# Low parts of weights used last on every tile, and new durations in the planner of a two-layer decoder trunk

## The chip, the cores and the metric

The kernel runs on one core of one Trainium2 chip, in one launch. The metric is the time of an execution on the device in microseconds (us). Three runs of the kernel before took 1206.88, 1209.07 and 1210.11 us; the median is 1209.07 us. The profile is of one more execution.

## The reference

The reference computes two layers of a decoder trunk on 256 tokens of 1024 features in float32. In short:

```python
for l in range(2):
    ada = silu(c) @ ada_w[l] + ada_b[l]                  # 9 vectors of 1024: shift, scale, gate for three sublayers
    h = rms_norm(x, g[0]) * (1 + scale0) + shift0
    x = x + 0.5 * gate0 * ((silu(h @ Wg) * (h @ Wu)) @ Wo)          # 1024 -> 2 x 2816 -> 1024
    h = rms_norm(x, g[1]) * (1 + scale1) + shift1
    p = h @ mix_w_in[l]                                  # 1024 -> 3360
    y = concat(gated_deltanet(p[...]), native_sparse_attention(p[...]))
    x = x + gate1 * (y @ mix_w_out[l])
    h = rms_norm(x, g[2]) * (1 + scale2) + shift2
    x = x + 0.5 * gate2 * ((silu(h @ Wg2) * (h @ Wu2)) @ Wo2)
return rms_norm(x, final_g)
```

The first sublayer and the third are feed-forward layers, with weights of 1024 x 5632 and 2816 x 1024 each. The mixing in between has four heads of a gated delta rule (a short convolution along the tokens, decays, inverses of unit triangles) and eight heads of attention with three branches (compressed keys, selected blocks, a window). The vectors `ada` that set shift, scale and gate are called the conditioning below; their weights are 1024 x 9216 per layer.

## The kernel before

**Products in two parts.** Activations lie with features on partitions and the 256 tokens along a row. A float32 product is made of three fast ones: weights and activations are each split into a high part, rounded to float32r, and a low part, the rest of the subtraction, and high x high, high x low and low x high are added up in a bank of PSUM. The split of the weights is work at run time. Weights come in tiles of 128 x 1024 floats (512 KB; some are smaller) through ten slots `raw`. For each, `produce()` (its lines follow `def load`) makes the high part `hi` with a copy on ScalarE and the low part `lo` with a subtraction on VectorE. Four slots each are there for `hi` and `lo`, so that at most three tiles are split ahead of the one in use. `take()` hands a pair to the products, and keeps the stream going.

**The order of products within a tile.** `split_mm` (L1018) makes three products for one block of 128 x 128 weights: `wh` with the high activations, `wh` with the low ones, `wl` with the high ones. A tile of weights holds eight blocks (four blocks of rows by two feature blocks of the result; six in one tile of three of the feed-forward's output weights), and the three products of a block follow each other. `early_mm` (L1011), for products that do not wait for the norm, has another order of the same three (`wh`, `wl`, `wh`). `split_mm_nat` (L1211) is for projections with tokens on partitions: there the activations are the stationary operand and a row block of weights, up to 512 columns, is the moving one. Its order is high x `wh`, high x `wl`, low x `wh`. The callers are `first_unit`, `ffn_body` (both halves of a feed-forward layer), `nat`, `proj_t`, `main` (inside `mix_body`) and `mix_out`. Two feature blocks of a result share each weight tile, one after the other.

**After the products.** A pair of feed-forward features goes through `ffn_act` (Silu on ScalarE, a product on VectorE `av`, and a split into `aa` on both). Results of output projections are added to the residual `xT` on VectorE, and `norm_add` takes them into the next norm (squares, a sum `nS` on GpSimd, scaled copies `xh` and `xl`).

**The conditioning.** `ada_piece` works on a piece of 1024 x 512 weights, four loads of 512 KB: some of its eight rows are added up on VectorE (`ada`, multiply-adds of 128 x 512), the others are scaled on ScalarE and added on GpSimd (`adb`). The pieces have fixed places in the stream of weights (`ADA_AT`), between the layers' tiles.

**What sets the order.** The kernel is first recorded, not issued. A planner (class `Program`) gives each instruction an estimated duration (`estimate`, L321), walks forward through the recorded program along these times, and picks for each engine the ready instruction with the longest way to the end; tiles get their slots on the walk. A pass backward sets how late each instruction may start, and eight such passes take turns; the order with the earliest estimated end is issued. So the estimates set the order of all five queues, the loads on SyncE among them, and each queue is then worked off in that order. Products that write one bank keep their recorded order; products of different banks may be mixed by the planner. All instructions are issued at one line, L546, so the profile tells them apart by the names of their tiles.

The functions that the diff touches follow; in many of them it only takes comments away.

Of the kernel before, what the change touches and what calls it, by code (L numbers as in the profile page):

```python
# [17 lines left out]
T = 256  # L18
DEPTH = 2
# [28 lines left out]
def const_arrays():  # L48
    """Masks and index patterns that depend on the shapes alone."""
# [39 lines left out]
DMA_START, DMA_DONE, DMA_BYTES, DMA_RING = 1100, 950, 360.0, 8  # L89
REUSE = {"tensor": 94, "vector": 220, "scalar": 300, "gpsimd": 250, "sync": 0}  # L90
PE_FIX, PE_WINDOW = 2.33, 4096 / 1.2
TABLE_LOAD, TABLE_BIAS = 1280, 5000
PASSES = 8
# [16 lines left out]
class Instr:  # L110
    """A recorded instruction."""
# [20 lines left out]
class LogicalTile:  # L132
    """A tile of the recorded program: one use of one of the slots of its tag."""
# [85 lines left out]
def wait_end(engine, end, other):  # L219
    """When an engine may reuse the place of a tile that another was done with at end."""  # L220
# [5 lines left out]
class Program:  # L226
# [8 lines left out]
    # -- recording --  # L235
# [17 lines left out]
    def region(self, ap):  # L253
        """(tile, first partition, end, bits of the columns)"""
# [21 lines left out]
    def record(self, engine, fn, args, kw):  # L276
# [6 lines left out]
        for w, r in sorted((u for u in uses if u[1]), key=lambda u: u[0]):  # L283
# [21 lines left out]
        if engine == "tensor":  # L305
            # products keep their order within a bank, as one start flag may stand for several of them
# [14 lines left out]
    def estimate(self, x):  # L321
        """Sets the time that the instruction holds its engine, and that of its transfer."""
# [3 lines left out]
        x.table, x.transfer = None, 0  # L326
        if x.fn == "dma_start":
            size = 4 * out.shape[0] * n
            run = min([size] + [4 * a.ap[-1][1] for a in aps])
            x.transfer = size / DMA_BYTES / min(1, run / 512)  # L330
            x.cost = 475
        elif x.engine == "tensor":
# [1629 lines left out]
```

## Time and profile before

| what | value |
|---|---|
| median of three runs | 1209.07 us (1206.88 to 1210.11) |
| span of the profiled execution, first to last instruction | 1203.7 us (its whole time is not listed) |
| tensor engine, products | 1160.3 us busy, 96%, 9450 products |
| tensor engine, weight loads | 1080.6 us, 90% |
| VectorE | 958.1 us, 80% |
| ScalarE | 669.8 us, 56% |
| GpSimd | 219.6 us, 18% |
| DMA | 259.89 MB, mean 216 GB/s |
| mean granted clock of the tensor engine | 0.995 |

Products are pipelined: one of 256 columns is listed with some 283 ns, while the next starts after some 117 ns. So their count in a stretch says more than the busy time. Weight loads run ahead of their products, and a product that has to wait shows first as a weight load that waits. A wait is put down to the operation that ended last before it.

### The profile page before, as it was taken

Reading aid. Unit: us, or ns where it says so; the run is one execution under the profiler, and the core shown is the slowest. Engines: PE = TensorE matmul, PEld = TensorE weight load, DVE = VectorE, ACT = ScalarE, POOL = GpSimd, SP = SyncE. Lnnn points to the kernel's source line nnn. Section 1 sums busy time; section 2 is a strip of 40 time slices with the busy share of each in tenths; the row PEclk is TensorE's granted clock in tenths of the full one; section 3 lists DMA queues with packets and bytes.
Section 4 is the critical chain, followed back from the end, with each engine's and each line's share of the span. In section 5 each row is a group of like instructions: output and inputs, shape, how many; then the busy total and the mean of one; then the engine's idle time right before and its main releaser. Section 6 shows DMA issues by size and latency. Waiting matters only on the chain.

```text
span 1203.7 us, 24132 instructions
## 1 busy us (share of the span) xinstructions
PE 1160.3 (96%) x9450; PEld 1080.6 (90%) x9451; DVE 958.1 (80%) x1716; ACT 669.8 (56%) x1177; POOL 219.6 (18%) x184
## 2 busy tenths in 40 slices
PE   8998989999999999999999999999999999999997
PEld 3698989997988899999999999998797879999997
DVE  3699899898987699988978877999998669855543
ACT  2456446555585556556545454556657556644444
POOL 2033343220001233113221110233100013200001
PEclk9999999999999999999999999999999999999999
DMA  9879999985424378987976887988562235756540
GB/s 333 292 218 313 293 303 308 287 254 171 132 54 123 118 225 294 301 272 227 319 224 187 284 265 221 314 283 283 157 192 55 71 102 181 255 172 193 181 145 36
DMA packets 230758, 259.89 MB, mean 216 GB/s; under 512 B 16130, under 2 KB 190836, under 8 KB 230644
## 3 DMA queue, kind: packets, MB, share of 16 engines
q1 hardware_dynamic: 230644, 258.35, 68.0%
q8 instruction: 74, 1.21, 0.4%
q14 instruction: 40, 0.33, 0.1%
HBM read 256.09 MB, written 2.23 MB: 215 GB/s over the span
## 4 chain that ended last, share of the span: by engine, by line
PE 72%; DVE 16%; DMA 4%; issue 3%; ACT 3%; POOL 1%; DVEq 0%; POOLq 0%; ACTq 0%; SPq 0%
PE bank L546 72%; DVE lo L546 7%; DVE ada L546 2%; ACT hi L546 2%; DMA raw<-in_ffn_w_out_dram 1%; DMA raw<-in_ada_w_dram 1%; DVE qT L546 1%; DVE aa L546 1%; POOL adb L546 1%; DMA raw<-in_ffn_w_in_dram 1%; DMA w<-in_cmp_w_k_dram 1%; DVE av L546 0%; DVE hl L546 0%; DVE KL L546 0%; DVE Pt L546 0%
## 5 line engine op out<-in xcount | busy, mean ns | idle before, releaser
L546 DVE TENSOR_TENSOR lo<-raw,hi 128x1024 fp32r<-128x1024 f32 (+3 forms) x340 | 420.2, 1254 | 119.6 <-ACT hi L546 86.4
L546 ACT ACTIVATE hi<-raw 128x1024 fp32r<-128x1024 f32 (+3 forms) x340 | 344.6, 1028 | 282.1 <-PE bank L546 233.2
L546 PE MATMUL bank<-hh,lo 128*128 128x256 f32 x1440 | 380.2, 285 | 10.4 <-DVE lo L546 10.3
L546 PE MATMUL bank<-hl,hi 128*128 128x256 f32 x1440 | 385.0, 284 | 0.6 <-DVE hl L546 0.6
L546 PE MATMUL bank<-hh,hi 128*128 128x256 f32 x1440 | 384.0, 283 | 1.6 <-ACT hi L546 1.0
L546 PEld LDWEIGHTS bank<-hh,lo 128*128 128x128 f32 x1440 | 260.2, 189 | 14.4 <-DVE lo L546 13.9
L546 PEld LDWEIGHTS bank<-hh,hi 128*128 128x128 f32 x1440 | 264.1, 189 | 4.7 <-issue 1.7
L546 PEld LDWEIGHTS bank<-hl,hi 128*128 128x128 f32 x1440 | 264.2, 189 | 1.2 <-DVE hl L546 0.8
L546 PE MATMUL bank<-aa,hi 128*128 128x256 f32 x1408 | 247.7, 281 | 2.9 <-ACT hi L546 2.5
L546 PEld LDWEIGHTS bank<-aa,hi 128*128 128x128 f32 x1408 | 212.5, 189 | 3.4 <-ACT hi L546 2.7
L546 PE MATMUL bank<-aa,lo 128*128 128x256 f32 x704 | 188.4, 283 | 8.5 <-DVE lo L546 8.5
L546 POOL TENSOR_TENSOR adb<-adb,raw 128x512 f32<-128x512 f32 x65 | 98.4, 1514 | 305.2 <-ACT raw L546 283.9
L546 PEld LDWEIGHTS bank<-aa,lo 128*128 128x128 f32 x704 | 129.5, 189 | 11.2 <-DVE lo L546 11.1
L546 DVE SCALAR_TENSOR_TENSOR ada<-raw,cond,ada 128x512 f32<-128x512 f32 x131 | 111.1, 848 | 4.5 <-DMA raw<-in_ada_w_dram 3.6
L546 POOL TENSOR_TENSOR nS<-nS,nsq 128x256 f32<-128x256 f32 x42 | 42.5, 1013 | 257.8 <-ACT nS L546 184.6
L546 ACT ACTIVATE aa<-av 128x256 fp32r<-128x256 f32 x88 | 36.0, 412 | 60.7 <-DVE av L546 60.5
L546 POOL TENSOR_TENSOR ada<-ada,adb 128x512 f32<-128x512 f32 x28 | 49.7, 1773 | 104.6 <-DVE ada L546 100.6
L546 PE MATMUL bank<-xl,hi 128*128 128x258 f32 (+1 forms) x224 | 62.3, 293 | 1.3 <-DVE xl L546 1.2
L546 PE MATMUL bank<-xh,hi 128*128 128x258 f32 (+1 forms) x224 | 60.5, 289 | 2.1 <-ACT xh L546 2.1
L546 PE MATMUL bank<-xh,lo 128*128 128x258 f32 (+1 forms) x224 | 61.4, 288 | 0.0
L546 DVE TENSOR_TENSOR aa<-av,aa 128x256 fp32r<-128x256 f32 x88 | 48.5, 554 | 10.9 <-ACT aa L546 10.9
L546 PEld LDWEIGHTS bank<-xl,hi 128*128 128x128 f32 x224 | 41.6, 190 | 7.1 <-issue 4.2
(308 smaller groups left out, 1620.9 us busy)
## 6 DMA issues: line engine op xcount, KB each, us to landing
raw<-in_ffn_w_in_dram SPq DMA_DIRECT2D x172, 512.0 KB, 4.8
raw<-in_ada_w_dram SPq DMA_DIRECT2D x144, 512.0 KB, 4.9
raw<-in_ffn_w_out_dram SPq DMA_DIRECT2D x64, 512.0 KB, 4.6
raw<-in_mix_w_in_dram SPq DMA_DIRECT2D x40, 512.0 KB, 5.0
raw<-in_ffn_w_out_dram SPq DMA_DIRECT2D x32, 384.0 KB, 4.3
raw<-in_mix_w_out_dram SPq DMA_DIRECT2D x8, 512.0 KB, 4.2
raw<-in_mix_w_out_dram SPq DMA_DIRECT2D x16, 256.0 KB, 4.5
raw<-in_mix_w_in_dram SPq DMA_DIRECT2D x8, 408.0 KB, 3.8
```

Of the source, the lines that this page charges most:

```text
L546: r = getattr(getattr(self.tc.nc, x.engine), x.fn)(*map(bind, x.args), **{k: bind(a) for k, a in x.kw.items()})
```

## The change

The diff does three things; it also takes the comments and docstrings of the file away.

First, all products of a weight tile with its high part come before all products with its low part. `split_mm`, `early_mm` and `split_mm_nat` go; `split_products` and `early_products` take a list of jobs for a tile.

Second, `estimate` has other figures: of a transfer (a fixed time per packet and a rate, over 16 engines), of a float32r product (2.2 instead of 2.4 columns per ns), of operations on GpSimd.

Third, the walk forward has three new surcharges: up to 500 ns on a vector operation with two inputs of more than 64 elements on chip while GpSimd is busy by the plan; 100 ns on a product after the tensor engine was idle; 95 ns on a product that uses another number of the array's columns than the one before.

```diff
-DMA_START, DMA_DONE, DMA_BYTES, DMA_RING = 1100, 950, 360.0, 8
+DMA_START, DMA_DONE, DMA_RING = 1100, 950, 8
+PACKET, PACKET_BYTES = 8, 23.5
+REFILL, DIVIDE, SHARED = 100, 95, 500
 ...
-        x.table, x.transfer = None, 0
+        x.table, x.transfer, x.cols = None, 0, 128
+        x.port = (x.engine == "vector" and not psum and sum(free_size(a) > 64 for a in aps[1:]) > 1)
 ...
-            x.transfer = size / DMA_BYTES / min(1, run / 512)
+            x.transfer = size / run * (PACKET + run / PACKET_BYTES) / 16
 ...
-                x.cost = PE_FIX + max(m / 1.2, w / 2.4)
+                x.cost = PE_FIX + max(m / 1.2, w / (2.2 if aps[1].dtype == F32R else 2.4))
+            x.cols = out.shape[0] if x.fn != "transpose" else 128
 ...
-            x.cost = 164 * n + 300 if x.kw.get("op") == OP.pow else 2.1 * n + 150
+            x.cost = 230 * n + 250 if x.kw.get("op") == OP.pow else 2.6 * n + 250
 ...
+            if x.port and clock["gpsimd"] > at:
+                cost += min(SHARED, clock["gpsimd"] - at)
             if x.engine == "tensor":
+                cost += (REFILL if at > clock["tensor"] + 20 else 0) + (DIVIDE if x.cols != cols else 0)
+                cols = x.cols
 ...
-    def split_mm(o, wh, wl, xh, xl, first, last):
-        PE.matmul(o, wh, xh, start=first, stop=False, skip_group_check=True)
-        PE.matmul(o, wh, xl, start=False, stop=False, skip_group_check=True)
-        PE.matmul(o, wl, xh, start=False, stop=last, skip_group_check=True)
+    def split_products(jobs):
+        for o, wh, _, xh, xl, first, _ in jobs:
+            PE.matmul(o, wh, xh, start=first, stop=False, skip_group_check=True)
+            PE.matmul(o, wh, xl, start=False, stop=False, skip_group_check=True)
+        for o, _, wl, xh, _, _, last in jobs:
+            PE.matmul(o, wl, xh, start=False, stop=last, skip_group_check=True)
 ...
+    def early_products(jobs, n=T + 2):
+        for o, wh, _, k in jobs:
+            PE.matmul(o[:, 0:n], wh, nst["xh"][:, k, 0:n], start=k == 0, stop=False)
+            PE.matmul(o[:, 0:n], wh, nst["xl"][:, k, 0:n], start=False, stop=False)
+        for o, _, wl, k in jobs:
+            PE.matmul(o[:, 0:n], wl, nst["xh"][:, k, 0:n], start=False, stop=k == KT - 1)
 ...
-                    for j in range(2):
-                        o, cs = qs[j][:, s * 256:(s + 1) * 256], slice(j * 128, (j + 1) * 128)
-                        for k in range(4):
-                            split_mm(o, wh[:, k, cs], wl[:, k, cs], hh[:, 4 * h + k], hl[:, 4 * h + k],
-                                     h == 0 and s == 0 and k == 0, h == 1 and k == 3)
+                    cut = [slice(j * 128, (j + 1) * 128) for j in range(2)]
+                    split_products([(qs[j][:, s * 256:(s + 1) * 256], wh[:, k, cut[j]], wl[:, k, cut[j]], hh[:, 4 * h + k],
+                                     hl[:, 4 * h + k], h == 0 and s == 0 and k == 0, h == 1 and k == 3)
+                                    for j in range(2) for k in range(4)])
```

The other callers change in the same way.

## Rows read from the trace of the kernel before

**Rows 1.** The page: span, tensor engine's busy time, the chain that ended last.
```profile
span 1203.7 us, 24132 instructions
PE 1160.3 (96%) x9450; PEld 1080.6 (90%) x9451; DVE 958.1 (80%) x1716; ACT 669.8 (56%) x1177; POOL 219.6 (18%) x184
...
PE 72%; DVE 16%; DMA 4%; issue 3%; ACT 3%; POOL 1%; DVEq 0%; POOLq 0%; ACTq 0%; SPq 0%
```
**Rows 2.** Stretches: length, busy us (count) per engine, clock, DMA share, GB/s.
```profile
60.00:210.00 150.00, 140.28 (x1158) 137.28 (x1157) 139.24 (x206) 84.43 (x132) 54.27 (x33) 0.98 0.89 287
210.00:420.00 210.00, 203.69 (x1697) 184.38 (x1696) 176.11 (x422) 128.61 (x272) 29.12 (x32) 1.00 0.55 163
420.00:600.00 180.00, 175.92 (x1462) 172.58 (x1461) 162.71 (x230) 103.54 (x160) 43.45 (x31) 1.00 0.84 272
600.00:840.00 240.00, 233.77 (x1946) 229.83 (x1946) 198.19 (x273) 128.90 (x197) 46.42 (x36) 1.00 0.81 257
...
1050.00:1170.00 120.00, 120.00 (x1023) 119.84 (x1022) 64.01 (x83) 56.77 (x81) 0.00 (x0) 1.00 0.57 176
```
**Rows 3.** Waits: us, times, longest; whole span, then 60:210, 210:600, 600:1050.
```profile
PE bank L546 <- DVE lo L546: 19.1, 26, 2.1
PEld bank L546 <- DVE lo L546: 25.7, 32, 2.3
PEld bank L546 <- ACT hi L546: 4.3, 4, 2.7
...
PEld bank L546 <- DVE lo L546: 8.8, 9, 1.8
PEld bank L546 <- DVE lo L546: 7.2, 9, 2.3
PEld bank L546 <- DVE lo L546: 8.6, 13, 1.1
```
**Rows 4.** Groups by shape: count, busy us, mean ns, idle before.
```profile
L546 DVE TENSOR_TENSOR lo<-raw,hi 128x1024 fp32r<-128x1024 f32 x292 | 372.3, 1292 | 100.0 <-ACT hi L546 73.3 <-PE bank L546 16.8 <-ACT aa L546 3.8
```
**Rows 5.** Groups by shape: what follows a finished bank at a layer's end.
```profile
L546 DVE SCALAR_TENSOR_TENSOR xT<-bank,gate,xT 128x256 f32<-128x256 f32 x32 | 15.0, 471 | 11.4 <-PE bank L546 11.2
L546 ACT ACTIVATE xh<-xT,am 128x256 fp32r<-128x256 f32 x48 | 22.3, 497 | 7.9 <-DVE xT L546 7.1 <-DVE am L546 0.8
```
**Rows 6.** Groups by shape: GpSimd's additions of the conditioning.
```profile
L546 POOL TENSOR_TENSOR adb<-adb,raw 128x512 f32<-128x512 f32 x65 | 98.4, 1514 | 305.2 <-ACT raw L546 283.9 <-DMA raw<-in_ffn_w_in_dram 15.4 <-issue 3.0
```
**Rows 7.** Timeline of VectorE from 168 us: start, duration.
```profile
168.17 1.52 DVE L546 TENSOR_SCALAR ada<-raw,cond 128x512 f32<-128x512 f32 x1
...
171.05 1.77 DVE L546 SCALAR_TENSOR_TENSOR ada<-raw,cond,ada 128x512 f32<-128x512 f32 x1
172.75 0.41 DVE L546 TENSOR_TENSOR av<-sg,bank 128x256 f32<-128x256 f32 x1
173.08 0.74 DVE L546 SCALAR_TENSOR_TENSOR ada<-raw,cond,ada 128x512 f32<-128x512 f32 x1
173.74 0.47 DVE L546 TENSOR_SCALAR ada<-raw,cond 128x512 f32<-128x512 f32 x1
```
**Rows 8.** Timeline of ScalarE from 173 us; in brackets the idle time before.
```profile
173.19 0.42 ACT L546 ACTIVATE aa<-av 128x256 fp32r<-128x256 f32 x1 [3.16 <-DVE av L546]
...
173.78 1.05 ACT L546 ACTIVATE hi<-raw 128x1024 fp32r<-128x1024 f32 x1
```
**Rows 9.** Timeline of the tensor engine from 174 us.
```profile
174.88 0.50 PE L546 MATMUL bank<-aa,hi 128*128 128x256 f32 x2 [2.48 <-ACT hi L546]
...
177.09 0.58 PE L546 MATMUL bank<-hh,lo 128*128 128x256 f32 x1 [1.59 <-DVE lo L546]
```
**Rows 10.** Slices of 5 us from 170 us, columns as in rows 2.
```profile
170.00:175.00 5.00, 2.52 (x22) 2.31 (x21) 5.00 (x7) 1.66 (x4) 3.23 (x3) 1.00 0.51 135
175.00:180.00 5.00, 3.41 (x16) 3.21 (x17) 5.00 (x8) 0.00 (x0) 0.34 (x1) 0.54 1.05 343
180.00:185.00 5.00, 5.00 (x42) 4.85 (x40) 3.48 (x5) 3.88 (x7) 0.95 (x1) 0.78 1.08 359
```

More of the change, by code (lines that the diff above doesn't have):

```diff
@@ L451, in forward @@
         window, cold, busy = 0, True, {}
+        cols = 128
         while len(order) < len(self.instrs):
@@ L1009, in norm_modulate @@
         return hh, hl
-    def early_mm(o, wh, wl, k, n=T + 2):
-        xh, xl = nst["xh"][:, k, 0:n], nst["xl"][:, k, 0:n]
-        PE.matmul(o[:, 0:n], wh, xh, start=k == 0, stop=False)
-        PE.matmul(o[:, 0:n], wl, xh, start=False, stop=False)
-        PE.matmul(o[:, 0:n], wh, xl, start=False, stop=k == KT - 1)
-    def split_mm(o, wh, wl, xh, xl, first, last):
-        PE.matmul(o, wh, xh, start=first, stop=False, skip_group_check=True)
-        PE.matmul(o, wh, xl, start=False, stop=False, skip_group_check=True)
-        PE.matmul(o, wl, xh, start=False, stop=last, skip_group_check=True)
+    def early_products(jobs, n=T + 2):
[10 more added lines that the diff above has]
+            PE.matmul(o, wl, xh, start=False, stop=last, skip_group_check=True)
     def ffn_act(f, g, bias, up, ah, al):
@@ L1046, in first_unit @@
                 wh, wl = take(("fi", l, i, u), 2 * h + s)
-                for k in range(4):
-                    for j in range(2):
-                        cs = slice(j * 128, (j + 1) * 128)
-                        early_mm(qs[j][s], wh[:, k, cs], wl[:, k, cs], 4 * h + k, T if startup else T + 2)
+                cut = [slice(j * 128, (j + 1) * 128) for j in range(2)]
+                early_products([(qs[j][s], wh[:, k, cut[j]], wl[:, k, cut[j]], 4 * h + k) for k in range(4) for j in range(2)],
+                               T if startup else T + 2)
         gu = tmp([128, 2, 2, T], F32, "gu")
@@ L1092, in ffn_body @@
                     wh, wl = take(("fi", l, i, u), 2 * h + s)
-                    for j in range(2):
-                        o, cs = qs[j][:, s * 256:(s + 1) * 256], slice(j * 128, (j + 1) * 128)
-                        for k in range(4):
-                            split_mm(o, wh[:, k, cs], wl[:, k, cs], hh[:, 4 * h + k], hl[:, 4 * h + k],
-                                     h == 0 and s == 0 and k == 0, h == 1 and k == 3)
+                    cut = [slice(j * 128, (j + 1) * 128) for j in range(2)]
+                    split_products([(qs[j][:, s * 256:(s + 1) * 256], wh[:, k, cut[j]], wl[:, k, cut[j]], hh[:, 4 * h + k],
+                                     hl[:, 4 * h + k], h == 0 and s == 0 and k == 0, h == 1 and k == 3)
+                                    for j in range(2) for k in range(4)])
             for j in range(2):
@@ L1107, in ffn_body @@
                     wh, wl = take(("fo", l, i, u, kh), c)
-                    for j in range(2):
-                        cs = slice(j * 128, (j + 1) * 128)
-                        for k in range(a, b):
-                            f = kh * 11 + k
-                            split_mm(qs[j][:, 0:256], wh[:, k - a, cs], wl[:, k - a, cs], ah[f], al[f], f == 0, f == NF - 1)
+                    cut = [slice(j * 128, (j + 1) * 128) for j in range(2)]
+                    split_products([(qs[j][:, 0:256], wh[:, f - kh * 11 - a, cut[j]], wl[:, f - kh * 11 - a, cut[j]], ah[f], al[f],
+                                     f == 0, f == NF - 1) for j in range(2) for f in range(kh * 11 + a, kh * 11 + b)])
             for j in range(2):
@@ L1203, in nat @@
                 wh, wl = take((tag, l), j)
+                tok = [slice(b * 128, (b + 1) * 128) for b in range(2)]
                 for k in range(2):
                     for b in range(2):
-                        t = slice(b * 128, (b + 1) * 128)
                         kk = 2 * j + k
-                        split_mm_nat(qs[b][:, :n], hh[:, kk, t], hl[:, kk, t], wh[:, k], wl[:, k], kk == 0, kk == KT - 1)
-            return qs
-        def split_mm_nat(o, xh, xl, wh, wl, first, last):
-            PE.matmul(o, xh, wh, start=first, stop=False)
-            PE.matmul(o, xh, wl, start=False, stop=False)
-            PE.matmul(o, xl, wh, start=False, stop=last)
+                        PE.matmul(qs[b][:, :n], hh[:, kk, tok[b]], wh[:, k], start=kk == 0, stop=False)
+                        PE.matmul(qs[b][:, :n], hl[:, kk, tok[b]], wh[:, k], start=False, stop=False)
+                for k in range(2):
+                    for b in range(2):
+                        kk = 2 * j + k
+                        PE.matmul(qs[b][:, :n], hh[:, kk, tok[b]], wl[:, k], start=False, stop=kk == KT - 1)
+            return qs
         def proj_t(tag, j):
@@ L1219, in proj_t @@
                 wh, wl = take((tag, l), 2 * j + h)
-                for c in range(2):
-                    o = q[:, c * 256:(c + 1) * 256]
-                    for k in range(4):
-                        cs = slice(c * 128, (c + 1) * 128)
-                        split_mm(o, wh[:, k, cs], wl[:, k, cs], hh[:, 4 * h + k], hl[:, 4 * h + k],
-                                 h == 0 and c == 0 and k == 0, h == 1 and k == 3)
+                cut = [slice(c * 128, (c + 1) * 128) for c in range(2)]
+                split_products([(q[:, c * 256:(c + 1) * 256], wh[:, k, cut[c]], wl[:, k, cut[c]], hh[:, 4 * h + k], hl[:, 4 * h + k],
+                                 h == 0 and c == 0 and k == 0, h == 1 and k == 3) for c in range(2) for k in range(4)])
             return q
@@ L1258, in main @@
                     wh, wl = take(("k", l), 2 * h + j)
-                    for k in range(4):
-                        for c in range(2):
-                            early_mm(qs[2 * j + c], wh[:, k, c * 128:(c + 1) * 128], wl[:, k, c * 128:(c + 1) * 128], 4 * h + k)
+                    cut = [slice(c * 128, (c + 1) * 128) for c in range(2)]
+                    early_products([(qs[2 * j + c], wh[:, k, cut[c]], wl[:, k, cut[c]], 4 * h + k) for k in range(4) for c in range(2)])
             rb = nst.pop("rbs")
@@ L1860, in mix_out @@
                 wh, wl = take(("mo", l, u), j)
-                for c in range(2):
-                    cs = slice(c * 128, (c + 1) * 128)
-                    for k in range(4):
-                        split_mm(qs[j][:, c * 256:(c + 1) * 256], wh[:, k, cs], wl[:, k, cs], yh[:, 4 * u + k], yl[:, 4 * u + k],
-                                 u == 0 and c == 0 and k == 0, u == 1 and k == 3)
+                cut = [slice(c * 128, (c + 1) * 128) for c in range(2)]
+                split_products([(qs[j][:, c * 256:(c + 1) * 256], wh[:, k, cut[c]], wl[:, k, cut[c]], yh[:, 4 * u + k], yl[:, 4 * u + k],
+                                 u == 0 and c == 0 and k == 0, u == 1 and k == 3) for c in range(2) for k in range(4)])
                 if u == 0:
```

## The prediction

> **What bounds the kernel now.** I read the page first. The tensor engine is busy 1160.3 of 1203.7 us, so 43.4 us is all the time in which it shows nothing to do; the chain that ended last is 72% tensor engine and 16% vector engine [rows 1]. The reader should see that two engines share the bound: a gain can come from the 43.4 us, and only where the vector engine is not the limit itself.
>
> Then the stages. From 1050 to 1170 us, with no conditioning work left, the tensor engine runs 1023 products in 120.00 us, without a gap: 117 ns a product [rows 2]. That is its pace when everything arrives. From 60 to 210 us it makes 1158 products where 150/0.117 = 1282 would fit; there the vector engine is busy 139.24 of 150 us and the DMA engines 0.89 of the time at 287 GB/s. From 420 to 600 us it makes 1462 of 1538, with the vector engine at 162.71 of 180. From 600 to 840 us, 1946 of 2051, the vector engine at 198.19 of 240. The mixing stage (210 to 420 us) has other shapes, so its count says nothing, but its idle time, 6.3 us, is small.
>
> Then the waits. The weight loads, which go ahead of each product, waited 25.7 us for the low parts of weights, 32 times, the longest 2.3 us, and only 4.3 us for the high parts; the products' own share of the wait for low parts is 19.1 us [rows 3]. By stretch the low parts cost 8.8 us (60 to 210), 7.2 us (210 to 600) and 8.6 us (600 to 1050); 1.1 us lies outside these.
>
> **The change: high parts first.** The same products run on the same tiles. No instruction and no byte is added or removed. Of a weight tile's 24 products the first that needs the low part was the third; it becomes the seventeenth. At 117 ns that is 14 x 0.117 = 1.64 us of extra cover for the subtraction that makes the low part, whose mean is 1292 ns [rows 4]. The output projection's tiles of three row blocks have 18 products, and gain 10 x 0.117 = 1.17 us; the token-major projections of the mixing have 12 longer ones, where the first low product moves from second to ninth. The mean wait is 25.7/32 = 0.80 us, so nearly every wait is shorter than the cover; of the longest, 2.3 us, about 0.7 us would stay. If each wait were an accident by itself, some 24 us would go: one end of the term. The other end is nothing: where the vector engine is full, the cover is used up once, the backlog grows on, and the next tile waits instead.
>
> I choose by stretch. From 60 to 210 us the vector engine has 7% to spare and the DMA 11%, so I credit 2 of 8.8 us. In the other two stretches and the remainder (7.2 + 8.6 + 1.1 = 16.9 us) the vector engine has 10 to 17% free, and the waits come singly, so I credit two thirds, 11 us. Term A: -13 us, between -24 and 0. What is late next is the high part: ScalarE's copies and the loads behind them. The high tile comes free after 16 products instead of 24, which helps that copy a little; the low tile and the raw tile come free no earlier.
>
> **What it moves to the end of a unit.** Two feature blocks share each weight tile. Before, the first block's bank was complete 12 products ahead of the second (9 in a tile of three row blocks); now it is 4 ahead (3). Its eviction starts 8 x 0.117 = 0.94 us (0.70 us) later, nearer to the second one's. Within a stage the next unit's products cover that. At the four ends of a feed-forward layer and the two of the output projection of the mixing the next norm waits for both blocks: the addition to the residual (471 ns) and the scaled copy (497 ns) of each now queue behind the other's [rows 5]. At most 4 x 0.70 + 2 x 0.94 = 4.7 us, at least nothing, as the first units of the next layer are started early. Term B: +2 us.
>
> **The estimates.** They cost no time on the chip by themselves; they change the planner's order on all queues, the loads on SyncE among them. The old figures are optimistic on each resource alike: a product 109 ns against 117 measured, now 118.7; a GpSimd addition of 512 columns 1225 ns against 1514 measured [rows 6], now 1581; a load of 512 KB in rows of 1 KB 1456 ns, now 512 x (8 + 1024/23.5)/16 = 1650 ns. Since the products and the loads all slow down by some 10%, most rankings should stay. What is new is the 500 ns that a vector operation with two large inputs on chip pays while GpSimd works.
>
> One place shows what that may be worth. At 171.05 us a multiply-add of the conditioning took 1.77 us, where the same one at 173.08 us took 0.74 [rows 7]; between them sat the product of a feed-forward feature, for which ScalarE waited 3.16 us in its own queue [rows 8], with the next high part behind it. The tensor engine then stood 2.48 us for that high part and 1.59 us for the next low part [rows 9]. After that idling the granted clock was 0.54 for a slice of 5 us, near the lower of its two levels (1.2 of 2.4 GHz), and 0.78 in the next; from 170 to 185 us there are 22 + 16 + 42 = 80 products where 15/0.117 = 128 would fit, 48 x 0.117 = 5.6 us lost [rows 10]. Of that 1.59 us is in term A. A planner that knows the price of the overlap would put the feature's product first. I credit half of the 4 us left, and nothing for all other reorderings, whose worth the trace of one order cannot show; the tensor engine's idle time that is not for low parts (43.4 - 19.1 = 24.3 us [rows 1, 3]) bounds their gain, and two more bursts of 5.6 us are the bound that I take for a loss. Term C: -2 us, between -24.3 and +11.2.
>
> A rule of the Trainium skill bears on this. The row at 168.17 us is a multiplication with one large input, and it took 1.52 us against 0.47 us for the same at 173.74 us [rows 7]; the planner's new surcharge goes to operations with two large inputs alone. The skill's page "SBUF — State Buffer", section "Who interferes with whom", says why both kinds can stretch: GpSimd shares a pair of ports with VectorE, a two-input operation and a one-input multiplication in a two-port mode both want it, and whoever starts first holds it for its whole instruction, so GpSimd is blocked as well. The trace agrees for VectorE, with 1.52 and 1.77 us. By that rule the new estimates still miss a part of the contention, and term C would be 0 instead of -2.
>
> **Sum.** -13 + 2 - 2 = -13 us on the profiled span of 1203.7 us, so a span of about 1190.7 us. The median of the runs, 1209.07, lies 5.4 us over that span (the page gives no other time of that execution); with the same 5.4 us on top, **1196 us**. With A between -18 and -6, B between 0 and +4 and C between -4 and +2, its own range is 1188 to 1204.
>
> **Rivals.**
> *The vector engine is the bound* (15%). The waits for low parts only move to later tiles. For it: 93% busy from 60 to 210 us [rows 2], and its 16% of the chain [rows 1]. Against it: from 600 to 840 us it has 17% free and the waits are as dear, 8.6 us from 600 to 1050. It would give about 3 us net: 1206, no change.
>
> *Slower: conditioning loads ahead of weights* (14%). The planner now thinks that a load of weights takes 13% longer, and reorders the loads. A piece of the conditioning is 4 loads of 512 KB, 2.1 MB; at 350 GB/s (343 and 359 in the fullest slices [rows 10]) it holds the weights behind it up by 6 us. It decides where the ten raw tiles on chip, 5.2 MB or 15 us of transfers, are full of such pieces when a feed-forward layer needs weights. For it: the DMA engines are 0.89 busy from 60 to 210 us, and 0.84 from 420 to 600 [rows 2]. Against it: weights that the tensor engine needs have the longer way to the end, and only 4.3 us are lost on high parts now [rows 3]. Three such pieces, 18 us, against the 13 gained: 1209 + 5 = 1214.
>
> *The order gets better everywhere* (13%). With right durations the in-order queues stop waiting behind operations that are late. For it: the burst at 170 us. It would take A at its end, -24, and C at -4, without B: 1181.
>
> **Numbers.** The forecast has 58%. The measurement can tell about 0.3%, 3.6 us: faster means under 1205.4, slower over 1212.7. Faster 0.58 + 0.13 = 0.71, the same 0.15, slower 0.14. The range leaves out the farther half of the third rival and most of the second: 1182 to 1211.
>
> **What would show it.** The weight loads' wait for low parts should fall from 25.7 us to under 13, most of the rest before 210 us; the waits for high parts should stay under 8 us; between 60 and 210 us the product count should rise from 1158 by no more than 50, between 600 and 840 us by about 50; no slice near 175 us should show a clock of 0.54. Waits of the weight loads for the scaled copies at the ends of layers should grow, by some 2 us. I am wrong if the low parts' wait falls and other waits of the same size replace it, or if the clock falls in more places.

## The result and the profile after

The changed kernel takes 1219.44 us (median of four runs, 1215.77 to 1220.31) against 1207.97 us for the kernel before in the same session: a ratio of 1.0092, 95% interval 1.0071 to 1.0112. It is slower by about 11 us. The forecast was 1196 us, and 1182 to 1211 with rivals, so it was wrong in sign and in range. The profiles below are of single executions: the changed kernel's took 1219.31 us, 1.8 us more than its span. If the same holds before, 3.6 of the 5.4 us that the forecast put on top of its span were a difference between executions.

The page of the changed kernel, with the lines that answer to [rows 1]:

```profile
span 1217.5 us, 24148 instructions
...
PE 1177.2 (97%) x9450; PEld 1088.9 (89%) x9451; DVE 955.5 (78%) x1716; ACT 672.7 (55%) x1177; POOL 219.7 (18%) x184
...
PE 75%; DVE 13%; DMA 6%; issue 2%; ACT 2%; POOL 1%; SPq 0%; DVEq 0%; POOLq 0%; ACTq 0%
```

The span is 13.8 us longer, and the tensor engine idles less, 40.3 instead of 43.4 us. It is listed as busy 16.9 us longer for the same 9450 products. So the loss does not show as idle time of the engine, which is where all the mechanisms that I had forecast would show it. By the listed lengths (some 283 ns for a product of 256 columns, 117 ns to the next) a wait under some 166 ns is counted as busy.

The stretches of [rows 2], with the same columns:

```profile
60.00:210.00 150.00, 142.99 (x1186) 140.03 (x1185) 143.20 (x209) 86.28 (x134) 56.19 (x34) 0.99 0.89 292
210.00:420.00 210.00, 204.36 (x1631) 179.02 (x1631) 171.62 (x415) 128.25 (x271) 27.88 (x33) 1.00 0.52 156
420.00:600.00 180.00, 177.10 (x1472) 173.53 (x1472) 157.42 (x228) 101.03 (x155) 37.66 (x28) 1.00 0.83 271
600.00:840.00 240.00, 233.89 (x1930) 229.35 (x1930) 192.38 (x266) 128.08 (x193) 49.91 (x36) 0.99 0.79 255
...
1050.00:1170.00 120.00, 120.00 (x1014) 119.84 (x1014) 69.36 (x94) 56.98 (x83) 1.29 (x1) 1.00 0.62 196
```

From 60 to 210 us there are 28 products more than before, and from 1050 to 1170 us the pace is nearly the same, 120/1014 = 118 ns a product. From 210 to 420 us there are 66 fewer. From 600 to 840 us, where I had expected about 50 more, there are 16 fewer.

The waits of the weight loads, as in [rows 3]:

```profile
PEld bank L558 <- issue: 35.3, 120, 0.8
PEld bank L558 <- DVE lo L558: 13.8, 26, 1.2
...
PEld bank L558 <- ACT hi L558: 5.7, 8, 1.2
PEld bank L558 <- POOL nS L558: 5.0, 4, 2.2
```

The low parts cost 13.8 us instead of 25.7. "Issue", where nothing that the profile shows was awaited, is the largest row. It was so before, with a line that [rows 3] leaves out:

```profile
PEld bank L546 <- issue: 28.1, 86, 1.7
```

It grew by 7.2 us, all in the two mixing stages (17.8 us before, 25.2 after), and `nS` grew by 4.7 us from 0.3. Together that is as much as the low parts' wait fell.

I then cut both traces at places that mean the same in each: the start of the last output product of a layer's first feed-forward part (tiles `aa`), and the start of the last product of the mixing's output projection (tiles `yh`, `yl`). The two mixing stages of the kernel before:

```profile
250.11:424.15 174.04, 170.20 (x1416) 151.28 (x1415) 144.59 (x388) 112.34 (x252) 17.18 (x24) 1.00 0.46 134
821.80:1002.44 180.64, 176.22 (x1414) 152.21 (x1413) 148.29 (x384) 115.55 (x256) 23.53 (x22) 1.00 0.47 138
```

and of the changed one:

```profile
240.61:424.44 183.83, 178.22 (x1416) 152.93 (x1415) 148.31 (x394) 114.60 (x255) 18.90 (x26) 1.00 0.44 132
820.62:1015.45 194.83, 187.04 (x1415) 157.88 (x1413) 154.05 (x393) 117.04 (x258) 25.36 (x24) 0.97 0.43 130
```

The mixing went from 174.0 + 180.6 = 354.7 us to 183.8 + 194.8 = 378.7 us, 24.0 us more. All the rest went from 849.0 to 838.9 us, 10.1 us less, 9.5 of these in the first feed-forward layer. The number of products in the two stages is the same (2830 and 2831); the tensor engine's listed busy time in them rose by 18.8 us and its idle time by 5.1 us.

The granted clock is 0.97 in the second of these stages, 1.00 before. It stood at 0.50, the lower of its two levels (1.2 of 2.4 GHz), from 824.6, 851.9 and 903.1 us for 3.4 us each; in the 4 us ahead of each the engine was busy 2.3 to 2.7 us. At half speed 10.2 us cost at most 5.1 us, an estimate.

A part of the longer busy time can be seen in one group, the products of the attention's probabilities with the values. They use 64 of the array's 128 columns. Before:

```profile
L546 PE MATMUL bank<-pt,vp 128*64 128x128 f32 x192 | 20.7, 287 | 2.1 <-ACT pt L546 2.1
```

After:

```profile
L558 PE MATMUL bank<-pt,vp 128*64 128x128 f32 x192 | 28.8, 293 | 0.0
```

192 products of 64 columns occupy 8.1 us more. The timeline of the tensor engine in the first mixing stage shows what stands between them. Before:

```profile
359.88 0.65 PE L546 MATMUL bank<-pt,vp 128*64 128x128 f32 x6
360.46 0.70 PE L546 MATMUL bank<-qT,kT 128*128 128x256 f32 x2
361.09 0.43 PE L546 MATMUL bank<-pt,vp 128*64 128x128 f32 x2
361.45 0.49 PE L546 MATMUL bank<-qT,kT 128*128 128x128 f32 x2
361.87 0.66 PE L546 MATMUL bank<-pt,vp 128*64 128x128 f32 x8
362.46 0.81 PE L546 MATMUL bank<-qT,kT 128*128 128x256 f32 x3
```

After:

```profile
354.34 0.38 PE L558 MATMUL bank<-hl,hi 128*128 128x256 f32 x1
354.66 0.43 PE L558 MATMUL bank<-pt,vp 128*64 128x128 f32 x2
355.02 0.39 PE L558 MATMUL bank<-hh,hi 128*128 128x256 f32 x1
355.24 0.39 PE L558 MATMUL bank<-qT,kT 128*128 128x128 f32 x2
355.56 0.43 PE L558 MATMUL bank<-pt,vp 128*64 128x128 f32 x2
355.92 0.33 PE L558 MATMUL bank<-CC,vT 128*128 128x128 f32 x1
356.01 0.37 PE L558 MATMUL bank<-hl,hi 128*128 128x256 f32 x1
356.21 0.27 PE L558 MATMUL bank<-CC,vT 128*128 128x128 f32 x1
356.41 0.43 PE L558 MATMUL bank<-pt,vp 128*64 128x128 f32 x2
356.78 0.33 PE L558 MATMUL bank<-CC,vT 128*128 128x128 f32 x1
```

Before, value products come in runs of six, two and eight: the eight from 361.87 us hand over after 0.59 us. After, pairs stand between single products of 128 columns: the pair at 354.66 us takes 0.36 us until the next product starts, and the one product ahead of it 0.32 us instead of 0.12. Counted along the two mixing stages, two neighbouring products use a different number of columns 175 times before and 217 times after. From start to start these pairs sum to 40.6 us before and 50.8 us after. That is 10.2 of the 24.0 us; the other 13.8 us are in pairs with the same number of columns.

### The profile page after: what moved, and what is told of

The parts are those of the page before. It is cut to its first block, busy times and chain, and to the rows that moved or that the text cites. A ratio compares the mean times of both kernels' runs of the same rounds, so it can differ in the third digit from the quotient of the medians.

```text
span 1217.5 us, 24148 instructions
## 1 busy us (share of the span) xinstructions
PE 1177.2 (97%) x9450; PEld 1088.9 (89%) x9451; DVE 955.5 (78%) x1716; ACT 672.7 (55%) x1177; POOL 219.7 (18%) x184
## 4 chain that ended last, share of the span: by engine, by line
PE 75%; DVE 13%; DMA 6%; issue 2%; ACT 2%; POOL 1%; SPq 0%; DVEq 0%; POOLq 0%; ACTq 0%
PE bank L558 75%; DVE lo L558 6%; DMA raw<-in_ada_w_dram 4%; DVE ada L558 1%; DVE Pt L558 1%; DMA Pt<-nd 1%; ACT hi L558 1%; POOL nS L558 1%; DVE aa L558 1%; DMA raw<-in_ffn_w_in_dram 0%; DMA raw<-in_ffn_w_out_dram 0%; DVE QS L558 0%; DVE qT L558 0%; SPq L558 0%; DVE av L558 0%
## 5 line engine op out<-in xcount | busy, mean ns | idle before, releaser
L558 PE MATMUL bank<-hh,hi 128*128 128x256 f32 x1440 | 354.2, 286 | 5.3 <-ACT hi L558 2.8
L558 PE MATMUL bank<-hl,hi 128*128 128x256 f32 x1440 | 351.0, 285 | 1.2 <-DVE hl L558 1.2
L558 PE MATMUL bank<-hh,lo 128*128 128x256 f32 x1440 | 254.3, 285 | 5.2 <-DVE lo L558 4.9
L558 PEld LDWEIGHTS bank<-hh,lo 128*128 128x128 f32 x1440 | 208.6, 189 | 9.7 <-DVE lo L558 8.1
L558 PE MATMUL bank<-aa,hi 128*128 128x256 f32 x1408 | 210.8, 282 | 1.9 <-ACT aa L558 0.8
L558 PEld LDWEIGHTS bank<-aa,hi 128*128 128x128 f32 x1408 | 188.5, 189 | 3.0 <-ACT aa L558 1.2
L558 PE MATMUL bank<-aa,lo 128*128 128x256 f32 x704 | 129.3, 284 | 2.7 <-DVE lo L558 2.6
L558 DVE SCALAR_TENSOR_TENSOR ada<-raw,cond,ada 128x512 f32<-128x512 f32 x131 | 111.3, 851 | 11.7 <-DMA raw<-in_ada_w_dram 11.0
L558 PEld LDWEIGHTS bank<-aa,lo 128*128 128x128 f32 x704 | 104.2, 188 | 5.2 <-DVE lo L558 4.6
L558 DVE TENSOR_TENSOR aa<-av,aa 128x256 fp32r<-128x256 f32 x88 | 45.9, 525 | 10.7 <-ACT aa L558 10.5
L558 ACT ACTIVATE raw<-raw,cond 128x512 f32<-128x512 f32 x65 | 44.4, 711 | 7.4 <-DMA raw<-in_ada_w_dram 7.2
L558 PE MATMUL bank<-xh,lo 128*128 128x258 f32 (+1 forms) x224 | 46.0, 290 | 0.0
```

Of the source, the lines that this page charges most:

```text
L558: r = getattr(getattr(self.tc.nc, x.engine), x.fn)(*map(bind, x.args), **{k: bind(a) for k, a in x.kw.items()})
```

## The experiments

Three theories. **A**: the order of products (low parts last) hurts the mixing. **B**: the new durations reorder it. **C**: the order of before was a lucky one, and any other order from the planner is slower. All times are medians; ratios are to the kernel before in the same session, with 95% intervals where there were three rounds. "Mixing" is the sum of the two stages cut as above.

**Parts alone.** The old durations with the new order of products:

```diff
-DMA_START, DMA_DONE, DMA_RING = 1100, 950, 8
+DMA_START, DMA_DONE, DMA_BYTES, DMA_RING = 1100, 950, 360.0, 8
 ...
-REFILL, DIVIDE, SHARED = 100, 95, 500
+REFILL, DIVIDE, SHARED = 0, 0, 0
 ...   # and the old formulas of transfer, float32r product and GpSimd
```

> High parts first everywhere, with the planner's estimates of before. The two mixing stages took 174 and 181 us before and 184 and 195 us after the change; the feed-forward layers got 11 us shorter in sum. Theory A (the order of products is what hurts the mixing: with low parts last the tensor engine's queue there gets worse, whatever the durations): the time stays at 1213 to 1221 us, the mixing at 182 or more and 190 or more. Theory B (the new durations reorder the mixing): the mixing goes back to about 174 and 181 us, the feed-forward gain stays, 1193 to 1201 us.

Measured: 1218.56 us, ratio 1.0092 (1.0077 to 1.0107), mixing 367.1. The time is as theory A had it; of the mixing's stages only the first is, with 186.1 us, and the second is as before, with 181.0. The gain outside of the mixing is gone as well (849.5 us against 849.0). One more thing was not expected: the low parts are still waited for.

```profile
PEld bank L558 <- DVE lo L558: 22.8, 29, 1.9
```

The new durations with the products in turn:

```diff
+    def split_in_turn(jobs):
+        for o, wh, wl, xh, xl, first, last in jobs:
+            PE.matmul(o, wh, xh, start=first, stop=False, skip_group_check=True)
+            PE.matmul(o, wh, xl, start=False, stop=False, skip_group_check=True)
+            PE.matmul(o, wl, xh, start=False, stop=last, skip_group_check=True)
 ...   # early_in_turn and nat likewise; all callers use these
```

> The new estimates and surcharges, with the three products of each block in turn as before. Theory A: mixing near 174 and 181 us, no gain in the feed-forward layers, 1204 to 1211 us. Theory B: mixing near 184 and 195 us and no gain in the feed-forward layers, 1218 to 1232 us. The waits of the weight loads for low parts should be near 25 us by both.

Measured: 1212.75 us, ratio 1.0050 (1.0031 to 1.0069), mixing 366.3. Between the two theories' ranges; slower without any new order of products, so B holds in part. The profiled execution, with 1216.54 us, is the slowest of the four, and its clock stood at the lower level for 13.6 us of the mixing, worth at most 6.8 us (estimate, half of the time).

```profile
PEld bank L558 <- DVE lo L558: 25.3, 37, 2.0
```

Then the order of products changed in the feed-forward layers alone. With the new durations (only the mixing's callers use the products in turn):

> As the changed kernel, but in the mixing (its three kinds of projections and its output projection) the three products of a block stay in turn. Theory A: mixing near 174 and 181 us with the feed-forward gain kept, 1193 to 1201 us. Theory B: mixing near 184 and 195 us, 1215 to 1222 us.

Measured: 1203.64 us, 0.9972 (0.9957 to 0.9987), mixing 360.2. A little faster than before, nearer to A than to B. With the old durations:

> High parts first in the feed-forward layers alone, with the old estimates. Both theories: mixing near 174 and 181 us. If the feed-forward gain of 11 us comes from the order, 1195 to 1200 us; if it comes from the estimates, 1206 to 1210 us.

Measured: 1221.14 us, 1.0105 (1.0088 to 1.0122), mixing 366.4, the rest 858.2. Neither case. Here not a line of the mixing or of the durations differs from before, and yet the mixing takes 11.7 us longer. This profile, too, is of the slowest of four executions (1226.47 us): its mixing stages have a clock of 0.96 and 0.98, 20.4 us at the lower level, worth at most 10.2 us by the same estimate. The 14 us by which the median is over before's are not explained by that alone, as the other three executions have a clock of 0.988 to 0.992 against 0.991 to 0.997 before. One order per kernel is not enough to compare kernels that a planner arranges; that led to the next group.

**Other orders of the same kernel.** A fixed number between 0 and 20 ns per instruction is added to the planner's rank:

```diff
-        x.boost = self.boost
+        x.boost = self.boost + (len(self.instrs) * 2654435761 + 1 * 40503) % 65536 / 65536 * 20
```

Of the kernel before, three such orders (1, 2 and 3 in the place of the first 1 behind the sum):

> The kernel before, unchanged but for a number between 0 and 20 ns, fixed per instruction, that is added to the planner's rank, which reaches to a million ns; it breaks near-ties another way. Theory C (the order of before was a lucky or tuned draw, and any other order from the same planner is slower): 1213 to 1225 us, the two mixing stages together 362 us or more instead of 354.6. Theories A and B (the changed parts themselves make the mixing slower): 1204 to 1211 us, mixing 350 to 359 us.

> The same with other numbers of that size. Theory C: 1213 to 1225 us, mixing 362 us or more. Theories A and B: 1204 to 1211 us, mixing 350 to 359 us.

> The same with other numbers of that size. Theory C: 1213 to 1225 us, mixing 362 us or more. Theories A and B: 1204 to 1211 us, mixing 350 to 359 us.

Measured: 1206.63, 1200.43 and 1194.56 us, mixing 357.9, 349.1 and 352.6. Theory C falls: the order of before is rather one of the slower ones. Of the changed kernel:

> The changed kernel with 0 to 20 ns per instruction added to the planner's rank, as in the first of the kernels of before with such numbers. Orders of the kernel before drawn in this way took 1207, 1200 and 1195 us beside its own 1207. If the change itself makes orders slower: 1210 us or more for all three of these, mean near 1216, mixing together 368 us or more. If the change only drew an unlucky order: 1195 to 1216 us with a mean near 1203, mixing 348 to 372 us.

> The same with the second set of numbers. The change is slower by itself: 1210 us or more. An unlucky order: anywhere from 1195 to 1216 us.

> The same with the third set of numbers. The change is slower by itself: 1210 us or more. An unlucky order: anywhere from 1195 to 1216 us.

Measured: 1223.01, 1219.50 and 1218.87 us, mixing 375.4, 374.2 and 376.8. With the first order of each, the kernel before has a mean of 1202.4 us over four orders and the changed one 1220.2; the mixing has 353.6 and 376.3, and no order of one comes near those of the other. The rest of the program is 844.6 and 842.5 us. So the loss is the change's own, about 18 us over orders (17 by the ratios to the kernel before in each session), and lies in the mixing. The lower clock does not make it: with half of the time at the lower level taken off each mixing, the means are 351.9 and 373.3 us, and the orders with number 2, with a clock of 1.00 in all four stages, have 349.1 and 374.2. The gain of 10.1 us outside of it was mostly the luck of one order: over four it is 2 us. Nor is the share of the column changes one of a single order: the pairs across a change sum to 38.3 us before and 51.9 after (means of four), 13.6 of the 22.7 us; the value products take 19.4 to 20.7 us in all four orders before and 28.6 to 28.8 in all four after.

A second order for each part alone:

> High parts first everywhere with the old estimates, in a second order (0 to 20 ns added to the planner's rank). If the order of products is a cause, mixing 363 us or more together and 1210 us or more, as in the first order (367 us, 1218.6). If that was one bad draw, 358 us or less and 1195 to 1208 us.

Measured: 1221.51 us, mixing 370.0.

> The new estimates with the products in turn, in a second order. If the estimates are a cause, mixing 363 us or more and 1208 us or more, as in the first order (366 us, 1212.8). If that was one bad draw, 358 us or less and 1195 to 1207 us.

Measured: 1211.46 us, mixing 359.9: the time as a cause had it, the mixing between the two cases. Over two orders each, the order of products alone costs 17.6 us against the mean of before, the durations alone 9.7 us. The order of products is a cause by these times. For the durations 9.7 us is less than the 13 us by which orders of one kernel differ, so two orders make it likely and no more. Neither part alone does what both do to the columns: there are 192 and 180 changes of column count with the order of products, 174 and 169 with the durations, 147 to 175 before and 217 to 232 with both.

**The changes of column count.** The planner's rank of a product loses 2000 ns where its column count differs from that of the product before:

```diff
-                            key=lambda c: c[1].way + c[1].boost - TABLE_BIAS * switch(c[1]) - IDLE * (c[0] - at))
+                            key=lambda c: c[1].way + c[1].boost - TABLE_BIAS * switch(c[1]) - IDLE * (c[0] - at)
+                            - 2000 * (c[1].engine == "tensor" and c[1].cols != cols))
```

In the changed kernel:

> The changed kernel, where the planner's rank of a product loses 2000 ns if it uses another number of the array's columns than the product before it on the tensor engine. In the mixing stages the changed kernel changes that number 217 times against 175 before, and spends 8.2 us more on such pairs. If these changes of columns are a cause of the loss, they fall to under 150, and the mixing goes from 183.8 and 194.8 us to about 177 and 187: 1202 to 1208 us. If the loss is only waits for other engines in an unlucky order, the count falls and the time stays at 1213 to 1225 us.

Measured: 1197.10 us, 0.9909 (0.9883 to 0.9934), 102 changes in the mixing instead of 217, mixing 355.9. More than was expected. In the kernel before (which gets `cols` as well, and no surcharge):

> The kernel before, where the planner's rank of a product loses 2000 ns if it uses another number of the array's columns than the one before it; durations and products as before. It has 175 such pairs in the mixing. If these pairs cost by themselves, wherever they come from, they fall to under 120 and the mixing from 354.6 to about 348 us: 1197 to 1203 us. If only the changed kernel suffers from them: 1204 to 1210 us.

Measured: 1186.64 us, 0.9818 (0.9799 to 0.9836), 99 changes instead of 175, mixing 340.8. It is faster than both kernels by far, and by more than was expected. Its mixing stages:

```profile
248.90:419.70 170.80, 167.46 (x1414) 151.06 (x1413) 145.46 (x389) 112.00 (x253) 16.22 (x25) 0.99 0.48 137
813.80:983.80 170.00, 165.19 (x1414) 149.76 (x1413) 147.05 (x384) 114.17 (x256) 23.70 (x22) 0.99 0.49 145
```

and those of the changed kernel with the same rank:

```profile
241.64:413.76 172.12, 166.50 (x1414) 150.72 (x1413) 148.17 (x390) 114.06 (x253) 18.49 (x25) 0.99 0.48 140
814.07:997.86 183.79, 174.28 (x1415) 154.43 (x1413) 151.66 (x394) 115.72 (x259) 24.90 (x24) 0.96 0.47 138
```

The value products of this kernel:

```profile
L550 PE MATMUL bank<-pt,vp 128*64 128x128 f32 x192 | 13.6, 280 | 1.4 <-ACT pt L550 1.4
```

and of the changed kernel with the same rank:

```profile
L559 PE MATMUL bank<-pt,vp 128*64 128x128 f32 x192 | 14.7, 282 | 1.7 <-ACT pt L559 1.7
```

From 20.7 and 28.8 us both are now near 14. The reader should see that the tensor engine was "busy" all along in time that could be saved. In both kernels what is saved in the mixing stands in the pairs across a change: they sum to 22.6 us (40.6 without the rank) and 23.7 us (50.8), while all other pairs take some 4 us more in each. The waits "issue" of the weight loads fall with them, from 28.1 and 35.3 to 18.0 and 18.9 us. The two other corners of the square, each part alone with this rank:

> High parts first with the old estimates, the planner keeping to a column count. The corners of the square known so far: neither part 1186.6 us, both parts 1197.1. If the order of products costs beside the column changes: 1194 us or more, mixing 350 us or more (340.8 with neither part). If the estimates make the rest: 1184 to 1189 us.

Measured: 1200.96 us, 0.9940 (0.9924 to 0.9957), mixing 348.1.

> The new estimates with the products in turn, the planner keeping to a column count. If the estimates cost beside the column changes: 1194 us or more, mixing 350 us or more. If the order of products makes the rest: 1184 to 1189 us.

Measured: 1195.80 us, 0.9906 (0.9885 to 0.9928), mixing 347.3. So with most of the column changes out of the way 10.5 us of loss remain (1197.10 against 1186.64), nearly all of the 11.5 us between the two kernels as they were, and either part alone makes about as much or more: 14.3 and 9.2 us. In the mixing the loss falls from 24.0 to 15.1 us, and of these only 1.1 us are left in pairs across a change; the other 14 us are in pairs of one column count, as 13.8 us were without the rank, and have not gone. The parts alone make 7.3 and 6.5 us there, just under what was expected of a cause. All four kernels became faster by 17 to 22 us with this rank, more than the 13 us by which orders of one kernel differ. The differences among the four, from single orders each, are hardly so.

**Who spends the cover.** The plan of the kernel before is kept for all queues; afterwards the places that one weight tile's products hold on the tensor engine are refilled with the high parts first, where no eviction stands in between (186 of 292 tiles):

```diff
-        self.issue(self.schedule())
+        self.issue(self.low_last(self.schedule()))
 ...
+            new = sorted(mine, key=lambda x: (weight(x) is lo, at[x]))
+            spots = [at[x] for x in mine]
 ...   # a tile is left as it is where an operand would not be ready or a place would be reused
+            for x, n in zip(new, spots):
+                order[n], at[x] = x, n
```

> The kernel before, planned as it was; afterwards, for 186 of 292 weight tiles (where no eviction stands in between), the places of the tile's products are refilled, high parts first. Every other queue keeps its order. If the cover is worth something and the planner spends it: the waits of the weight loads for low parts fall from 25.7 to 12 us or less, mixing stays near 354.6, 1194 to 1202 us. If the cover is worth nothing: 1204 to 1211 us, with other waits in the place of those for low parts.

Measured: 1200.47 us, 0.9935 (0.9913 to 0.9956), mixing 357.9, the rest 843.4 instead of 849.0.

```profile
PEld bank L546 <- DVE lo L546: 12.8, 14, 2.0
...
PEld bank L546 <- ACT hi L546: 4.4, 7, 1.4
...
PEld bank L546 <- DVE av L546: 3.4, 2, 1.7
```

The waits for low parts are halved, from 25.7 us in 32 waits to 12.8 in 14, a little short of the 12 us expected, and the kernel is 6.5 us faster than before in its session (1206.93 us). Here the cover, on top of a plan made without it, is worth half of the waits that it takes away. The same on the kernel that keeps to a column count:

> The same refilling, of 183 of 292 tiles, on the kernel before whose planner keeps to a column count (1186.6 us). If the cover is worth something: waits for low parts from 28.3 to 14 us or less and 1174 to 1181 us. If not: 1184 to 1189 us.

Measured: 1185.81 us, 0.9810 (0.9787 to 0.9833). The waits fell as expected, from 28.3 us:

```profile
PEld bank L550 <- DVE lo L550: 11.2, 13, 1.6
```

But the time did not follow: it cannot be told from 0.9818. The rest fell from 843.9 to 839.3 us and the mixing rose from 340.8 to 344.4. Waits for high parts rose from 2.2 to 7.5 us.

## Why the prediction was wrong

**Term A (-13 us): right in its sign in this run, wrong in its mechanism.** The waits fell to 13.8 us, close to the "under 13" that I had named, and the first feed-forward layer got shorter by 9.5 us. But I took the cover of 1.64 us as a gift that stays, as if all other queues kept their order. It is a planner's input. With the order of products changed and the old durations the waits were 22.8 and 18.8 us, against 22.7 to 26.7 in the four orders of before; with both changes they were 13.8, 14.8, 16.0 and 20.6 us; with the same order of products laid over the old plan they were 12.8. So the planner gave back a part of the cover: over four orders 8.3 us of waits went (24.6 to 16.3), not 13. Nor did they go where I had said: from 60 to 210 us, where VectorE is fullest and I credited 2 us, 8.8 us became 3.3, and from 600 to 1050 us 8.6 became only 6.5. I also priced a microsecond of wait as a microsecond of time. Outside of the mixing the four orders gained 2 us, and in the two refilled kernels 12.9 and 17.1 us of waits gave 6.5 us and nothing clear of noise. Taking the k-th high part and the k-th low part of the trace, the low part was ready 2581 ns (mean) after the high one in the kernel before, 2865 ns in the refilled one, 3445 ns in the one planned with low parts last and old durations, and 3430 ns in the changed one. The row that answers to [rows 4] shows the same shift. After:

```profile
L558 DVE TENSOR_TENSOR lo<-raw,hi 128x1024 fp32r<-128x1024 f32 x292 | 372.8, 1288 | 102.1 <-PE bank L558 66.0 <-ACT hi L558 26.5 <-issue 4.4
```

Before, VectorE's idle time ahead of a subtraction ended mostly with its high part (73.3 of 100.0 us): it waited for it. Now it ends mostly with a product (66.0 of 102.1 us). A subtraction reads the raw and the high tile, so a product that it waits for is one that sets a low tile free. A low tile comes free at the end of its products, as before; the high one now comes free earlier, and the wait moved from one to the other. In the refilled kernel:

```profile
L546 DVE TENSOR_TENSOR lo<-raw,hi 128x1024 fp32r<-128x1024 f32 x292 | 371.9, 1291 | 90.1 <-ACT hi L546 46.5 <-PE bank L546 29.0 <-issue 5.8
```

it is in between. That the high tile comes free earlier I had named, but I put no price on it. What else the planner did with the cover is not shown.

**Term B (+2 us): not tested by itself, and its sign did not show.** The waits of the weight loads for the scaled copies `xh`, which I had expected to grow by some 2 us, fell from 3.9 to 0.8 us; those for the sum of squares `nS` at the ends of layers grew from 0.3 to 5.0 us. The refilled kernels leave tiles as they were where an eviction stands in between, so they do not test it.

**Term C (-2 us, between -24.3 and +11.2): the step that failed.** I wrote that the product durations and the loads all slow by some 10% so that most rankings should stay, and that the mixing's "other shapes" say nothing while "its idle time, 6.3 us, is small". I gave "nothing for all other reorderings", and no term at all to what the new order of products does to the plan. The mixing is where the new order decides. Its loss of 24.0 us in this run (22.7 over orders) is beyond my bound for a loss, 11.2 us, which I had set at two more bursts like the one at 175 us. Idle time was the wrong measure there: only 5.1 us of the 24.0 are listed as idle time.

About half of the loss is known: the new plan mixed products of 64 and 32 columns with those of 128. In pairs of neighbours with different column counts the time from start to start summed to 40.6 us before (175 pairs) and to 50.8 us after (217), 10.2 us more and not the 8.2 us that I name in an expectation above; over four orders it is 13.6 of 22.7 us. Keeping to a column count takes that part away, 24.0 us become 15.1. The rest stays, and its cause is open. The changed kernel's surcharge DIVIDE names the price of a change, but adds it to the plan's clock only after a product has been picked; it was not part of that choice, and the prediction has no term for it. The Trainium skill's page "TensorEngine Tiling (Array Packing)", section "Key Properties" under "Tiling Modes", states that changing the tiling mode, not only the tile, drains the engine. The traces here agree as far as a change costs time: 212 and 203 ns from start to start across a change between 128 and 64 columns, 119 ns between two products of 128; that it is a drain they do not show. The page gives no price.

**The signs.** The burst near 175 us did go. The slices that answer to [rows 10], and the one that is now the worst of that stretch:

```profile
160.00:165.00 5.00, 3.55 (x27) 3.34 (x26) 5.00 (x6) 2.38 (x5) 3.67 (x3) 0.74 1.01 344
170.00:175.00 5.00, 5.00 (x44) 5.00 (x44) 4.49 (x7) 3.71 (x7) 1.46 (x2) 1.00 1.04 352
175.00:180.00 5.00, 5.00 (x44) 5.00 (x44) 5.00 (x7) 2.74 (x5) 4.23 (x3) 1.00 1.05 361
```

From 170 to 180 us the clock stays at full speed with 88 products instead of 38; at 160 us it is 0.74 for a slice. But both signs of being wrong came: other waits of the same size stand in the place of the low parts' ("issue" and `nS`), and the clock falls in more places, three of them in the second mixing stage. The rule on the ports that I weighed ("SBUF — State Buffer", "Who interferes with whom" in the Trainium skill) stands undecided: no run here has its part alone.

**The slower rival (conditioning loads ahead of weights)** had the right sign at 1214 us and the wrong place: high parts are waited for 5.7 us instead of 4.3, and the stretch that it named first, 60 to 210 us, got faster. The other two rivals, 1206 and 1181 us, had no loss in the mixing either.

**What stays open.** Which of the planner's choices sets the mixing's column changes up when low parts come last is not shown; neither is what makes the remaining 10.5 us with columns kept, 15.1 us in the mixing. There the tensor engine's idle time is 15.1 us in the changed kernel and 8.1 in the other, and the clock in the second stage 0.96 and 0.99. The order with the feed-forward layers alone and the old durations (1221.14 us) is not explained either: it has 172 column changes in the mixing, 3 fewer than before.

## What to carry to other kernels

Where a planner arranges the queues, a change in the recorded order or in a duration is a new plan: compare several near-tie orders of each kernel (here their spread was 13 us for one kernel) before a difference of 1% is put down to the change. Cover that is given to a planner can be spent by it in part; laid over a finished plan it stays, though a wait that goes need not be time gained. Price a switching cost where the choice is made, not only in the clock of the plan, and do not take a busy tensor engine for one without slack.

## What the runs showed of the hardware

Products of 64 columns that follow each other, on alternating halves, started 58 ns apart (median of 220 in the mixing of the kernel before); a product of 64 columns after one of 128 started after 212 ns, and one of 128 after one of 64 after 203 ns, against 119 ns between two of 128 columns. I had not expected a planned order to lose as much by these changes: keeping to a column count took the kernel before from 1208.9 us (that session's median) to 1186.6 us, 22.3 us, while its waits for low parts were 28.3 us (25.7 without). Refilling, which halved these waits in the kernel before, gained 6.5 us.
